# A hybrid decoder layer in fp32 on one core: residual loaded early, raw weights cut four slots behind their loads, output operands in pieces, leftover scores finished beside the first value tiles

## The chip, the cores and the metric

The kernel runs on one core of one Trainium2 chip. The time is the device time of one execution in microseconds (us), and the smaller it is the better. Three executions took 1523.22, 1521.63 and 1522.43 us, with a median of 1522.43 us. A fourth execution was recorded by the hardware profiler; it took 1521.24 us, and its trace spans 1519.5 us. All rows that are shown below come from that one.

## The reference

One decoder layer works on `x` of 1024 tokens by 1024 columns, with 256 memory tokens. Everything is float32. Two groups of heads run side by side on the same normalized input, and their outputs are joined before one output projection:

```python
h = rmsnorm(x, ln1)
z = h @ w_in                       # 4 mLSTM heads of 128, 8 attention heads of 64
mq, mk = silu(causal_conv(ml_qk))  # mLSTM: chunks of 64 tokens with a carried state
ml_out = norm(mlstm_chunkwise(mq, mk, mv, ig, lf)) * ml_norm * sigmoid(ml_o)

def block(qi, ci, blk):            # forgetting attention, 128 queries at a time
    s = q @ k.T * scale + (c[:, None] - c[None, :])   # c: running sum of log forget gates
    s = where(qpos >= kpos, s, -inf)
    return softmax(s) @ v

x = x + concat([ml_out, fx_out]) @ w_out
x = x + cross_attention(rmsnorm(x, ln_x), rmsnorm(mem, ln_mem), w_xq, w_xkv, w_xo)
u = relu(rmsnorm(x, ln2) @ w_ff1)
x = x + (u * u) @ w_ff2
return rmsnorm(x, ln_f)
```

## The kernel before

**Tiling.** The 1024 tokens are held as two halves of 512. Every float32 operand of a large product is kept as two parts, a rounded high part and the rest (`split`, L138 on ACT for the high part, L139 on DVE for the rest), and each product is three matmuls (`mm3`, L192 to L194). Weights come from memory unsplit into a ring of two buffers called `wr` ("raw") and are then cut into `wh` and `wl`.

**Engines and queues.** PE multiplies and transposes. ACT, DVE and POOL do the element work. All DMAs are issued by the queue of SP, in order, and an issue that has to wait for its data or its buffer holds back those behind it. A scheduler places the instructions of each engine, except inside `in_order(...)`, where the order of the source is kept.

**The stage of the change.** It computes the forgetting attention of the 8 heads, and lies between about 355 and 590 us of the trace. Its loop is `slot()` (L998). Scores of a head come in parts of at most 512 keys for 128 queries. A part goes through four steps: `score` (two matmuls, L754 and L755, into one of three PSUM banks called `sc`, with a causal mask added by L734 in the next slot), `top` (the maximum, DVE L761), `exp` (ACT L767, and for a second part also L769) and `scale` (the division by the sum, POOL L778). A value tile goes through `turn` (up to four transposes on PE, L793), `cut` (split of the transposed tile, L138 and L139) and `add` (matmuls with the values, L813). Each head's values are read back from DRAM by `fv_load` (L856, tile `w` from `fvd`), where `fv_sink` has stored them (L664).

The first 13 slots (`LEAD_`) do score parts only, without values. Then comes `token_major(w_fv)`, the projection of the values, in two passes of eight token tiles. Then about 96 slots do one value tile each, and in source order: turn, mask of the last score, add of the tile of two slots ago, `top` of the last score part, `cut`, `exp` of the part before that, `scale`, one waiting load (`fx_step`, L728), the next `score`, a stretch of filler matmuls, and at most one half of a raw weight cut (`cut_half`: ACT L971, then L972 on POOL for the first half and on DVE for the second). A score part needs the bank of the part three before it, and so the `exp` of that part.

**The filler.** `units` is a list of products that need nothing of this stage: key units and value units of the cross-attention's memory tokens (operand `hm`, 2 MB, read from `hmd` at L1074), then out units, the part of the output projection that needs only the mLSTM heads and the first attention heads. `cut_half` cuts the raw weights of the units ahead, as soon as fewer than three are waiting; after the second half of a raw weight it issues the load of the next one (L959) into the buffer that came free. The residual (`kept`, the first half of `x`, eight pieces of 256 KB) and the output operands (`mix_ahead`) are loaded piece by piece by `fx_step`, from a list `coming` that `score_parts` fills head by head. The output operands of the last heads (`mix_fx`, L877) are loaded behind the slots, in transfers of 768 KB.

Of the kernel before, what the change touches and what calls it, by code (L numbers as in the profile page):

```python
# [9 lines left out]
F32 = mybir.dt.float32  # L10
F32R = mybir.dt.float32r
AF = mybir.ActivationFunctionType
ALU = mybir.AluOpType
# [6 lines left out]
TH = 512  # L20
D = 1024
KT = D // P
NM = 256
MLH = 4
FXH = 8
# [3 lines left out]
KX = 1  # L29
# [15 lines left out]
def hybrid_layer(ctx: ExitStack, tc: tile.TileContext, a: dict, out: bass.AP):  # L45
    nc = tc.nc
    v, s, g = nc.vector, nc.scalar, nc.gpsimd
# [14 lines left out]
    def act(dt=F32R):  # L62
        return sb("act", [P, 8, TH], 7, dt)
# [47 lines left out]
    load = nc.sync.dma_start  # L111
# [35 lines left out]
    @contextmanager  # L147
    def in_order(engines=COMPUTE):

        traced = nc.cur_bb.bb.instructions  # L150
        last = traced[-1]
        yield
        start = next(k for k in reversed(range(len(traced))) if traced[k] is last) + 1
        for i in traced[start:]:
            if i.engine not in engines:
                continue
            if i.engine in last_of:
                tc.add_manual_dep(
                    i,
                    last_of[i.engine],  # L160
                    mybir.DependencyInfo(mybir.DependencyClass.NoSync, mybir.DependencyReason.DATA),
                    reason="in_order",
                )
            last_of[i.engine] = i.name
# [120 lines left out]
    hmd = dram.tile([P, 2, KT, NM], F32, name="hmd")  # L285
# [217 lines left out]
    def token_major(w_src, sink, cs=(0, 1), between={}, ready=()):  # L503

        for c in cs:
            ws = [both(ready.pop(0) if ready else weights(w_src[c, i]), lambda t: t.rearrange("p (k c) -> p k c", k=4)) for i in range(2)]
            for t in range(8):
                if t in between:
                    between[t]()
                hf, tt = divmod(t, 4)  # L510
                ps = mm()[:, 0:256]
                for k in range(KT):
                    x = both(h[hf], lambda z: z[:, k, tt * P : (tt + 1) * P])
                    mm3(ps, x, both(ws[k // 4], lambda z: z[:, k % 4]), k == 0, k == KT - 1)
                sink(t, c, ps)
# [150 lines left out]
    closing = iter(())  # L666
# [45 lines left out]
    coming = []  # L712
# [121 lines left out]
    def score_parts():  # L834

        for hd in range(FXH):
            for hf in range(2):
                if hf:
                    t = act(F32).rearrange("p a b -> p (a b)").rearrange("p (i c) -> p i c", i=4)
                    rooms[hd, hf] = [t[:, d, : (5 + d) * P] for d in range(4)]  # L840
                else:
                    t = [w4((P, 2, TH)) for _ in range(2)]
                    rooms[hd, hf] = [t[d // 2][:, d % 2, : (1 + d) * P] for d in range(4)]
                for d in range(4):
                    x = Tile(hd, 4 * hf + d, rooms[hd, hf][d])
                    for e in range(len(x.parts)):
                        yield x, e
            if hd + 2 < FXH:
                fx_load(hd + 2)
            if hd == FXH - 2:  # L850
                extra[hd].extend(mix_ahead(1))
            coming.extend(extra[hd])

    def fv_load(hd):
        t = w4((P, 8, P), F32R)
        load(t.bitcast(F32), fvd[hd])  # L856
        return t

    def value_steps():
# [22 lines left out]
    def mix_ahead(hf):  # L882
        t = act().rearrange("p (e k) c -> p e k c", e=2)
        z = [z4()[:, :T].bitcast(F32R).rearrange("p (e c) -> p e c", e=2) for _ in range(KX)]
        mixes[hf] = [(t[:, 0, k], t[:, 1, k]) for k in range(MLH)] + [(y[:, 0], y[:, 1]) for y in z]
        return [(mixes[hf][k][p_], mix[hf, p_, :, k]) for k in range(MLH + KX) for p_ in range(2)]

    late = []

# [59 lines left out]
    units += [out_unit(hf, n) for hf in range(2) for n in range(KT)]  # L949

    sources = [(u, src) for u, (srcs, _) in enumerate(units) for src in srcs]
    raws_, cuts_, halves = [], {}, [0]

    def raw_load():
        n = len(raws_)
        if n < len(sources):
            src = sources[n][1]
            raw = sb("wr", [P, 1024], 2)[:, : src.shape[-1]]
            last_raw[:] = [load(raw, src)]  # L959
            raws_.append(raw)  # L960

    def cut_half():

        n, e = divmod(halves[0], 2)
        raw = raws_[n]
        c = raw.shape[-1]
        if e == 0:
            cuts_.setdefault(sources[n][0], []).append(tuple(sb(t, [P, 1024], 3, F32R)[:, :c] for t in ("wh", "wl")))
        hi, lo = cuts_[sources[n][0]][-1]
        c = slice(e * c // 2, (e + 1) * c // 2)  # L970
        s.activation(hi[:, c], raw[:, c], AF.Copy)  # L971
        (v if e else g).tensor_tensor(out=lo[:, c], in0=raw[:, c], in1=hi[:, c].bitcast(F32), op=ALU.subtract)  # L972
        halves[0] += 1
        if e:
            raw_load()
# [19 lines left out]

    stores, topped = [], []

    def slot(values, until):  # L998
        with in_order(COMPUTE + (mybir.EngineType.SP,) * (values or not until)):
            todo_ = late[:]  # L1000
            late.clear()
            closing = bool(ended)
            sums = []
            while ended:
                sums.append(fx_close(*ended[0]))
                hd, hf, _ = ended.pop(0)
                if hd % 2:
                    stores.append((hd, hf, True))
            x = next(steps_, None) if values else None
            if x:  # L1010
                x.turn()
            mask()

            while adds and not closing and len(adds) >= (LAG if x else 1):
                y = adds.pop(0)
                y.add()
                if y.last:
                    ended.append((y.hd, y.hf, y.ov))
                    break
            tops = scored[:]  # L1020
            scored.clear()
            for t, e in tops:
                t.top(e)
            if x:
                x.cut()
                adds.append(x)
            for f in sums:
                f()
            exps = topped[:]
            topped[:] = tops  # L1030
            for t, e in exps:
                t.exp(e)
            while exped:
                exped.pop(0).scale()
            exped.extend(t for t, e in exps if e == len(t.parts) - 1)
            fx_step()
            part = next(parts, None)
            if part:
                part[0].score(part[1])
                scored.append(part)  # L1040
            late.extend(filter(None, [f() for f in todo_]))
            if stores and stores[0][2]:
                stores[0] = (*stores[0][:2], False)
            elif stores:
                fx_store(*stores.pop(0)[:2])
            while spent[0] < until:
                step = next(fill, None)
                if step is None:
                    break
                spent[0] += step[0]  # L1050
                if step[1]:
                    late.append(step[2])
                    break
            n, e = divmod(halves[0], 2)
            if until and n < len(sources) and (e or sum(u >= now[0] for u, _ in sources[:n]) < 3):
                cut_half()
        return x

    fx_load(0)
# [3 lines left out]
    for i in range(LEAD_):  # L1063
        slot(False, 0)
        if i in (1, 11):
            next(closing, None)
    token_major(a["w_fv"], fv_sink, between={4: lambda: next(closing, None)})
    hm = act().rearrange("p a b -> p (a b)").rearrange("p (e k c) -> p e k c", e=2, k=KT)
    kept = act(F32)
    residual = [(kept[:, n], a["x"][:, n, :TH]) for n in range(KT)]  # L1070
    operands = mix_ahead(0)
    for hd, more in ((1, residual[:4]), (2, operands[:4]), (3, operands[4:8]), (4, operands[8:] + residual[4:6]), (5, residual[6:])):
        extra[hd].extend(more)
    load(hm.bitcast(F32), hmd)  # L1074
    banks[:] = ["mm", "m2"]
    raw_load()
    raw_load()
# [13 lines left out]
        if step[1]:  # L1091
            (step[2]() or (lambda: None))()
    banks[:] = ["mm", "tp", "m2", "tp"]
    mix_fx = [mix_load(MLH + KX, KT, hf) for hf in range(2)]
    h2 = [(act(), act()) for _ in range(2)]
    second_acc = [w2("b") for _ in range(2)]
    mix_done = []
# [636 lines left out]
```

## Time and profile before

| what | value |
|---|---|
| median of three executions | 1522.43 us (1521.63 to 1523.22) |
| the profiled execution, its span | 1521.24 us, 1519.5 us |
| PE busy | 1502.5 us, 99% of the span |
| DVE, ACT, POOL busy | 1103.0, 716.8 and 441.5 us |
| moved by DMA | 288.32 MB, mean 190 GB/s |
| mean granted clock of PE | 0.996 |
| PE busy in 40 us from 360, 400, 440, 480, 520, 560 us | 38.88, 38.77, 37.64, 39.37, 40.00, 39.72 us |

The profile has for each instruction its start, its duration, its line, and in brackets the idle time of its engine ahead of it with the instruction that ended it. Rows of matmuls overlap: the next begins before the row of the one before it ends. A row of `SPq` is the issue of a DMA by SP's queue, not the transfer. In the rows of windows, each engine has its busy time in us and its instructions in brackets, and the last three columns are the granted clock of PE (1.00 is full), the busy share of the 16 DMA engines, and GB/s.

### The profile page before, as it was taken

The page shows a single profiled execution, that of the slowest core. Times are in us where ns is not written, and L with a number is a line of the kernel's source. Part 1 is how long each engine was busy: PE and PEld are TensorE (multiplying, and loading weights), DVE is VectorE, ACT ScalarE, POOL GpSimd, SP SyncE. Part 2 cuts the span into 40 slices and gives each one's busy share as a digit, 9 for nine tenths or more (in the row PEclk, how much of TensorE's full clock was granted, in tenths as well). Part 3 has the DMA queues.
Part 4 walks back from the last instruction along what each step waited for, and adds up shares of the span by engine and source line. Part 5 has one row for each costly group of instructions (what it writes and reads, how often), then busy time and mean ns, then how long its engine had stood idle before and what let it go on. Part 6 is the DMA issues. An engine that isn't in the chain of part 4 may idle for free.

```text
span 1519.5 us, 21816 instructions
## 1 busy us (share of the span) xinstructions
PE 1502.5 (99%) x7708; PEld 1260.7 (83%) x7708; DVE 1103.0 (73%) x1741; ACT 716.8 (47%) x1345; POOL 441.5 (29%) x497
## 2 busy tenths in 40 slices
PE   9999999999999999999999999999999999999997
PEld 8888888889898887888888888788888788888887
DVE  7666676665798875844457888788887788777765
ACT  7343343334677763543443456566556432222134
POOL 0003030413455541011110033344333544343312
PEclk9999999999999999999999999999999999999998
DMA  6332333446788858634333436776776966565623
GB/s 212 117 114 87 120 103 116 132 128 180 229 263 241 246 162 320 219 105 131 126 108 127 162 124 241 271 277 238 272 253 214 364 260 221 222 221 218 253 84 111
DMA packets 115217, 288.32 MB, mean 190 GB/s; under 512 B 12818, under 2 KB 27468, under 8 KB 109476
## 3 DMA queue, kind: packets, MB, share of 16 engines
q1 hardware_dynamic: 114820, 286.82, 55.9%
q8 instruction: 60, 0.98, 0.3%
q14 instruction: 49, 0.40, 0.1%
q10 hardware_dynamic: 288, 0.11, 0.0%
HBM read 194.36 MB, written 92.53 MB: 189 GB/s over the span
## 4 chain that ended last, share of the span: by engine, by line
PE 61%; DVE 3%; DMA 2%; issue 1%; ACT 1%; POOL 1%; SPq 0%; POOLq 0%; DVEq 0%; ACTq 0%
PE sc L192 5%; PE sc L194 5%; PE sc L193 5%; PE tp L192 5%; PE tp L194 5%; PE tp L193 5%; PE m L192 4%; PE m L194 4%; PE m L193 4%; PE mm L192 4%; PE mm L193 4%; PE mm L194 4%; PE ov L192 2%; PE ov L194 2%; PE ov L193 2%; PE ov L813 1%
## 5 line engine op out<-in xcount | busy, mean ns | idle before, releaser
L193 PE MATMUL tp<-act,wh 128*128 128x512 f32 (+1 forms) x456 | 178.7, 392 | 0.0
L192 PE MATMUL tp<-act,wl 128*128 128x512 f32 (+1 forms) x456 | 178.5, 392 | 0.0
L194 PE MATMUL tp<-act,wh 128*128 128x512 f32 (+1 forms) x456 | 178.5, 392 | 0.0
L138 ACT ACTIVATE wh<-wr 128x1024 fp32r<-128x1024 f32 (+3 forms) x96 | 92.7, 966 | 97.5 <-PE tp L194 36.4
L192 PE MATMUL mm<-act,wl 128*128 128x512 f32 (+1 forms) x320 | 122.9, 384 | 0.3 <-DVE r_b L940 0.3
L193 PE MATMUL mm<-act,wh 128*128 128x512 f32 (+1 forms) x320 | 122.5, 383 | 0.0
L194 PE MATMUL mm<-act,wh 128*128 128x512 f32 (+1 forms) x320 | 122.2, 382 | 0.0
L192 PE MATMUL m<-act,wl 128*128 128x512 f32 (+1 forms) x312 | 119.7, 384 | 0.5 <-DVE wl L139 0.5
L139 DVE TENSOR_TENSOR wl<-wr,wh 128x1024 fp32r<-128x1024 f32 (+3 forms) x96 | 111.9, 1166 | 10.6 <-ACT wh L138 10.5
L194 PE MATMUL m<-act,wh 128*128 128x512 f32 (+1 forms) x312 | 119.1, 382 | 0.0
L193 PE MATMUL m<-act,wh 128*128 128x512 f32 (+1 forms) x312 | 118.9, 381 | 0.0
L192 PE MATMUL sc<-act,wl 128*128 128x512 f32 (+1 forms) x268 | 103.8, 387 | 0.0
L193 PE MATMUL sc<-act,wh 128*128 128x512 f32 (+1 forms) x268 | 103.6, 387 | 0.0
L194 PE MATMUL sc<-act,wh 128*128 128x512 f32 (+1 forms) x268 | 103.6, 387 | 0.0
L194 PEld LDWEIGHTS tp<-act,wh 128*128 128x128 f32 x456 | 85.7, 188 | 19.5
L192 PEld LDWEIGHTS tp<-act,wl 128*128 128x128 f32 x456 | 85.7, 188 | 18.9
L193 PEld LDWEIGHTS tp<-act,wh 128*128 128x128 f32 x456 | 85.8, 188 | 18.8
L1468 POOL TENSOR_TENSOR z<-wr 128x256 f32<-128x256 f32 x56 | 53.5, 975 | 146.7 <-DMA wr<-w_ff2q 119.0
L138 ACT ACTIVATE w<-wr 128x768 fp32r<-128x768 f32 (+2 forms) x31 | 25.5, 825 | 130.1 <-PE tp L194 69.0
L138 ACT ACTIVATE wh<-z 128x1024 fp32r<-128x1024 f32 (+2 forms) x55 | 52.5, 956 | 65.6 <-POOL z L1468 30.6
L139 DVE TENSOR_TENSOR wl<-z,wh 128x1024 fp32r<-128x1024 f32 (+2 forms) x55 | 67.3, 1223 | 11.3 <-ACT wh L138 11.3
L194 PEld LDWEIGHTS mm<-act,wh 128*128 128x128 f32 x320 | 60.1, 188 | 12.5
(673 smaller groups left out, 4205.3 us busy)
## 6 DMA issues: line engine op xcount, KB each, us to landing
act<-right SPq DMA_DIRECT2D x35, 1024.0 KB
right<-r_d SPq DMA_DIRECT2D x70, 256.0 KB
right<-w SPq DMA_DIRECT2D x56, 256.0 KB
wr<-w_ff2q SPq DMA_DIRECT2D x28, 512.0 KB
act<-fqk SPq DMA_DIRECT2D x48, 256.0 KB
wr<-w_in SPq DMA_DIRECT2D x20, 512.0 KB
wr<-w_ff SPq DMA_DIRECT2D x20, 512.0 KB
fqk<-r_p SPq DMA_DIRECT2D x32, 256.0 KB
```

What stands on the lines that cost most here:

```text
L138: s.activation(hi, src, AF.Copy)
L139: return v.tensor_tensor(out=lo, in0=src, in1=hi.bitcast(F32), op=ALU.subtract)
L192: nc.tensor.matmul(ps, w[1], x[0], start=first, stop=False, skip_group_check=more)
L193: nc.tensor.matmul(ps, w[0], x[1], start=False, stop=False, skip_group_check=more)
L194: nc.tensor.matmul(ps, w[0], x[0], start=False, stop=last, skip_group_check=more)
L813: nc.tensor.matmul(self.ov[:, c0:], self.fv[:, self.j], t[:, c0:], start=self.j == 0 and t is self.p[1], stop=self.last and t is self.p[0])
L1468: g.tensor_tensor(out=o, in0=x, in1=y, op=op)
```

## The change

There are six edits.

1. `score_steps` takes the steps `top`, `exp` and `scale` out of `slot`, and `catch_up` calls them without a new score, ahead of token tiles 0 and 2 in each of the two passes of `token_major(w_fv)`. The score parts that the first 13 slots leave unfinished get their mask, maximum, exponential and division there.
2. `raw_load` notes the slot in which a raw weight was asked for, and `slot` cuts it only from four slots later on (`SETTLE`). `cut_for`, which a unit calls when it begins, does not look at that.
3. The POOL half of `cut_half` becomes two instructions of half the width.
4. The residual is loaded as four pieces of 512 KB, put into `coming` right behind the projection of the values, instead of eight pieces of 256 KB among the loads of heads 1, 4 and 5.
5. `hm` is loaded in two halves of 1 MB; the second is issued behind the first `fv_load`.
6. The output operands of the last heads are taken into `coming` at the last head, eight pieces of 256 KB (`rest_ahead`); four pieces of 256 KB are left for the place where the transfers of 768 KB stood (`rest_last`).

```diff
+            if hd == FXH - 1:
+                extra[hd].extend(rest_ahead())
             coming.extend(extra[hd])
...
-        load(t.bitcast(F32), fvd[hd])
+        x = load(t.bitcast(F32), fvd[hd])
+        if hd == 0:
+            with tc.issue_after(x.ins):
+                load(hm[:, :, KT // 2 :].bitcast(F32), hmd[:, :, KT // 2 :])
...
+    def rest_ahead():
+        for hf in range(2):
+            mix_fx.append(act().rearrange("p (e k) c -> p e k c", e=2))
+        return [(mix_fx[hf][:, p_, k], mix[hf, p_, :, MLH + KX + k]) for hf in range(2) for k in range(KT - MLH - KX - 1) for p_ in range(2)]
+
+    def rest_last(hf):
+        k = KT - MLH - KX - 1
+        for p_ in range(2):
+            load(mix_fx[hf][:, p_, k].bitcast(F32), mix[hf, p_, :, MLH + KX + k])
+        return [(mix_fx[hf][:, 0, k], mix_fx[hf][:, 1, k]) for k in range(k + 1)]
...
+    SETTLE = 4
...
+            asked.append(slots[0])
...
-        (v if e else g).tensor_tensor(out=lo[:, c], in0=raw[:, c], in1=hi[:, c].bitcast(F32), op=ALU.subtract)
+        if e:
+            v.tensor_tensor(out=lo[:, c], in0=raw[:, c], in1=hi[:, c].bitcast(F32), op=ALU.subtract)
+        else:
+            m = c.stop // 2
+            for q in (slice(0, m), slice(m, c.stop)):
+                g.tensor_tensor(out=lo[:, q], in0=raw[:, q], in1=hi[:, q].bitcast(F32), op=ALU.subtract)
...
+    def score_steps():
+        tops = scored[:]
+        scored.clear()
+        for t, e in tops:
+            t.top(e)
+        yield
+        exps = topped[:]
+        topped[:] = tops
+        for t, e in exps:
+            t.exp(e)
+        while exped:
+            exped.pop(0).scale()
+        exped.extend(t for t, e in exps if e == len(t.parts) - 1)
+
+    def catch_up():
+        with in_order():
+            mask()
+            for _ in score_steps():
+                pass
...
-            if until and n < len(sources) and (e or sum(u >= now[0] for u, _ in sources[:n]) < 3):
+            if until and n < len(sources) and slots[0] >= asked[n] + SETTLE and (e or sum(u >= now[0] for u, _ in sources[:n]) < 3):
                 cut_half()
+            slots[0] += 1
...
-    token_major(a["w_fv"], fv_sink, between={4: lambda: next(closing, None)})
+    token_major(a["w_fv"], fv_sink, between={0: catch_up, 2: catch_up, 4: lambda: next(closing, None)})
...
-    residual = [(kept[:, n], a["x"][:, n, :TH]) for n in range(KT)]
+    coming.extend((kept[:, n : n + 2], a["x"][:, n : n + 2, :TH]) for n in range(0, KT, 2))
...
-    load(hm.bitcast(F32), hmd)
+    load(hm[:, :, : KT // 2].bitcast(F32), hmd[:, :, : KT // 2])
...
-    mix_fx = [mix_load(MLH + KX, KT, hf) for hf in range(2)]
+    mix_fx = [rest_last(hf) for hf in range(2)]
```

**ACT where the value slots begin.** A row is a line, an operation, what it writes, what it reads, and the shape; numbers behind names tell copies apart. L767 is the `exp` of a score part, L141 stores a value tile of the projection, L138 is the high part of a transposed tile. Before:

```order
L141 ACTIVATE r_p_3769<-mm_3744,rcol 128x4x64
L141 ACTIVATE r_c_3798<-tp_3773,rcol 128x4x64
L141 ACTIVATE r_b_3827<-m_585_3802,rcol 128x4x64
L138 ACTIVATE r_d_3850<-tp_3843 128x512
L767 ACTIVATE act_3246,c_den_3304<-sc_3311,c_mx_3303 128x512
L769 ACTIVATE c_mx_3303<-c_mx_3303 128x1
L138 ACTIVATE r_d_3868<-tp_3862 128x384
L767 ACTIVATE w_537_3329,c_den_3332<-sc_3333,c_mx_3331 128x128
```

The same place after the change:

```order
L141 ACTIVATE r_p_3780<-mm_3755,rcol 128x4x64
L767 ACTIVATE act_3246,c_den_3304<-sc_3311,c_mx_3303 128x512
L769 ACTIVATE c_mx_3303<-c_mx_3303 128x1
L767 ACTIVATE w_537_3329,c_den_3332<-sc_3333,c_mx_3331 128x128
L141 ACTIVATE r_c_3809<-tp_3784,rcol 128x4x64
L141 ACTIVATE r_b_3838<-m_585_3813,rcol 128x4x64
L138 ACTIVATE r_d_3860<-tp_3855 128x512
L138 ACTIVATE r_d_3876<-tp_3870 128x384
```

The last two leftover exponentials stand ahead of the last two tiles of the value projection, and no longer behind the first transposed tiles.

**ACT at the eleventh raw weight** (a half of `w_xv`; the high part of a raw weight is L971 before and L991 after). Before:

```order
L138 ACTIVATE r_d_4841<-tp_4829 128x512
L767 ACTIVATE act_4709,c_den_4785<-sc_4786,c_mx_4784 128x512
L971 ACTIVATE wh_4871<-wr_4765 128x512
L138 ACTIVATE w_832_4883<-tp_4875 128x512
L767 ACTIVATE act_4709,c_den_4785<-sc_4819,c_mx_4784 128x256
L769 ACTIVATE c_mx_4784<-c_mx_4784 128x1
L138 ACTIVATE r_a_4856<-r_a_4856 128x256
L971 ACTIVATE wh_4871<-wr_4765 128x512
```

The same place after the change:

```order
L138 ACTIVATE r_d_4852<-tp_4840 128x512
L767 ACTIVATE act_4718,c_den_4795<-sc_4796,c_mx_4794 128x512
L138 ACTIVATE w_830_4890<-tp_4882 128x512
L767 ACTIVATE act_4718,c_den_4795<-sc_4830,c_mx_4794 128x256
L769 ACTIVATE c_mx_4794<-c_mx_4794 128x1
L138 ACTIVATE r_a_4867<-r_a_4867 128x256
L991 ACTIVATE wh_4908<-wr_4775 128x512
L138 ACTIVATE r_d_4922<-tp_4913 128x384
```

The first half of that cut stands one slot later, behind the `exp` that it stood ahead of.

**SP's queue at the first load of values.** Before (L1074 loads `hm`, L664 stores values, L644 and L645 store attention operands, L261 and L637 are small rows of the mLSTM state):

```order
L664 DMA fvd<-r_c_3624 128x4x128
L856 DMA w_593_3840<-fvd 128x1024
L261 DMA r_a_3215<-facd 128x512
L637 DMA r_d_3216<-facd 128x512
L664 DMA fvd<-r_b_3653 128x4x128
L664 DMA fvd<-r_p_3682 128x4x128
L1074 DMA act_3831<-hmd 128x4096
```

The same part of the queue after the change, up to the second half of `hm`:

```order
L664 DMA fvd<-r_p_3693 128x4x128
L644 DMA mix<-r_y_3316 128x512
L1112 DMA act_3842<-hmd 128x2x1024
L644 DMA mix<-r_e_3475 128x512
L645 DMA mix<-r_f_3067 128x512
L645 DMA mix<-r_f_2932 128x512
L664 DMA fvd<-r_c_3722 128x4x128
L664 DMA fvd<-r_b_3751 128x4x128
L664 DMA fvd<-r_p_3780 128x4x128
L858 DMA w_593_3851<-fvd 128x1024
L861 DMA act_3842<-hmd 128x2x1024
```

The first load of values (L856, now L858) moves from behind the ninth store of values to behind the fourteenth.

More of the change, by code (lines that the diff above doesn't have):

```diff
@@ L886, in mix_ahead @@
         return [(mixes[hf][k][p_], mix[hf, p_, :, k]) for k in range(MLH + KX) for p_ in range(2)]
+    mix_fx = []
+    def rest_ahead():
[7 more added lines that the diff above has]
+        return [(mix_fx[hf][:, 0, k], mix_fx[hf][:, 1, k]) for k in range(k + 1)]
     late = []
@@ L951, in hybrid_layer @@
     sources = [(u, src) for u, (srcs, _) in enumerate(units) for src in srcs]
-    raws_, cuts_, halves = [], {}, [0]
+    raws_, cuts_, halves, asked, slots = [], {}, [0], [], [0]
+    SETTLE = 4
     def raw_load():
@@ L1019, in slot @@
                     break
[L1020 to L1023, printed above, removed]
+            going = score_steps()
+            next(going)
             if x:
@@ L1028, in slot @@
                 f()
[L1029 to L1035, printed above, removed]
+            next(going, None)
             fx_step()
@@ L1066, in hybrid_layer @@
             next(closing, None)
-    token_major(a["w_fv"], fv_sink, between={4: lambda: next(closing, None)})
+    token_major(a["w_fv"], fv_sink, between={0: catch_up, 2: catch_up, 4: lambda: next(closing, None)})
     hm = act().rearrange("p a b -> p (a b)").rearrange("p (e k c) -> p e k c", e=2, k=KT)
     kept = act(F32)
-    residual = [(kept[:, n], a["x"][:, n, :TH]) for n in range(KT)]
+    coming.extend((kept[:, n : n + 2], a["x"][:, n : n + 2, :TH]) for n in range(0, KT, 2))
     operands = mix_ahead(0)
-    for hd, more in ((1, residual[:4]), (2, operands[:4]), (3, operands[4:8]), (4, operands[8:] + residual[4:6]), (5, residual[6:])):
+    for hd, more in ((2, operands[:4]), (3, operands[4:8]), (4, operands[8:])):
         extra[hd].extend(more)
-    load(hm.bitcast(F32), hmd)
+    load(hm[:, :, : KT // 2].bitcast(F32), hmd[:, :, : KT // 2])
     banks[:] = ["mm", "m2"]
```

## The prediction

> **What bounds the kernel now.** I read the engines' busy times first.
>
> ```profile
> PE 1502.5 (99%) x7708; PEld 1260.7 (83%) x7708; DVE 1103.0 (73%) x1741; ACT 716.8 (47%) x1345; POOL 441.5 (29%) x497
> ```
>
> PE is busy for 1502.5 of 1519.5 us, and the change takes no matmul away. It can only win time in which PE stands idle or runs slowly, inside the stage that it touches. So next come PE's waits between 360 and 600 us (what waited, for what: us in total, times, longest) and three windows of that stretch.
>
> ```profile
> PE sc L754 <- ACT act L767: 3.1, 2, 2.4
> PE tp L793 <- DVE r_e L139: 1.5, 2, 0.9
> PE sc L754 <- ACT w L767: 0.4, 1, 0.4
> PE mm L192 <- DVE r_b L940: 0.3, 1, 0.3
> PE tp L793 <- DVE w L139: 0.3, 1, 0.3
> ```
>
> ```profile
> 360.00:400.00 40.00, 38.88 (x311) 36.77 (x310) 26.22 (x71) 21.69 (x58) 13.29 (x20) 1.00 0.87 259
> 400.00:440.00 40.00, 38.77 (x292) 36.31 (x291) 37.23 (x83) 31.84 (x87) 20.91 (x30) 1.00 0.67 202
> 440.00:480.00 40.00, 37.64 (x273) 35.39 (x272) 31.83 (x78) 29.17 (x84) 20.32 (x31) 0.96 0.88 251
> ```
>
> The waits add up to 5.6 us in seven stalls. A stall costs a little more than its bracket shows:
>
> ```profile
> 410.20 0.28 PE L193 MATMUL mm<-wl,act 128*128 128x256 f32 x1
> 410.32 0.28 PE L194 MATMUL mm<-wh,act 128*128 128x256 f32 x1
> 411.47 0.33 PE L793 MATMUL tp<-ident,act 128*128 128x128 f32 x1 [0.87 <-DVE r_e L139]
> ```
>
> The row of 410.20 lasts 0.28 us, but the next starts after 0.12. Without the stall the row of 411.47 would have started at 410.44, and it came 1.03 later: 0.16 more than shown. I add 0.16 to each stall, 7 x 0.16 = 1.1 in all. Only the third window has a clock below 1.00. Its cause is the one long stall:
>
> ```profile
> 449.50 0.53 SPq L959 DMA_DIRECT2D wr<-w_xv  x1
> 457.41 0.63 ACT L971 ACTIVATE wh<-wr 128x512 fp32r<-128x512 f32 x1 [4.31 <-DMA wr<-w_xv]
> 459.03 0.50 PE L754 MATMUL sc<-act 128*128 128x512 f32 x1 [2.36 <-ACT act L767]
> 460.00:461.00 1.00, 1.00 (x8) 1.00 (x7) 0.98 (x2) 1.00 (x3) 0.00 (x0) 0.52 0.00 0
> 461.00:462.00 1.00, 1.00 (x4) 0.81 (x4) 0.96 (x4) 0.87 (x4) 0.00 (x0) 0.50 1.12 295
> 462.00:464.00 2.00, 2.00 (x11) 1.81 (x11) 1.45 (x5) 0.84 (x4) 1.60 (x3) 0.64 0.80 255
> ```
>
> ACT, in its order, stands 4.31 us at a raw half whose load took 7.9 us from issue to use; PE waits 2.36 for the exponential behind it, and right after that runs at 0.52, 0.50 and 0.64. At full clock that work had needed 0.48 + 0.50 + 2 x 0.36 = 1.7 us less. So the most that the change can win is 5.6 + 1.1 + 1.7 = 8.4 us, 0.55%.
>
> **The change part by part.**
>
> *Leftover scores.*
>
> ```profile
> 392.36 0.68 ACT L767 ACTIVATE act<-sc,c_mx 128x512 f32<-128x512 f32 x1
> 393.18 0.44 PE L754 MATMUL sc<-act 128*128 128x384 f32 x1 [0.73 <-ACT act L767]
> 396.99 0.38 PE L754 MATMUL sc<-act 128*128 128x256 f32 x1 [0.39 <-ACT w L767]
> 385.00:390.00 5.00, 5.00 (x45) 5.00 (x44) 1.99 (x6) 1.18 (x4) 1.48 (x3) 1.00 1.03 348
> ```
>
> The first value slots each wait for an exponential of a part that was left over from the slots without values. The change puts these ahead of the last projection tiles, where ACT is busy for 1.18 of 5 us, so they cost nothing there. It frees 0.73 + 0.39 + 2 x 0.16 = 1.4. Ends: 1.4, and 0 if the wait goes to the next link of the same chain. I take 1.2, near the first, since ACT's next work in these slots is only the high part of a transposed tile.
>
> *Four slots between load and cut.* The 96 value slots lie between about 394 us and the last stall at 585 us (below): 2.0 us each. The cut of the eleventh raw weight moves one slot, 2.0 us, and ACT would then wait 4.31 - 2.0 = 2.3. In the trace 4.31 of ACT's waiting cost PE 2.36, so 1.95 are slack, and 0.35 + 0.16 = 0.5 stay. Stalls of 0.73 and 0.87 left the clock at 1.00 in their windows, so the 1.7 go too. The gain is 2.36 + 0.16 + 1.7 - 0.5 = 3.7. Its ends are 4.2 (the load comes sooner) and 0 (it comes later still). What speaks for sooner is that the transfers of the residual ahead of it are gone:
>
> ```profile
> 432.91 1.39 SPq L728 DMA_DIRECT2D act<-x  x3
> 400.00:405.00 5.00, 5.00 (x41) 4.71 (x39) 4.65 (x7) 4.70 (x13) 2.20 (x3) 1.00 0.40 123
> ```
>
> They now go at about 402 to 412 us, where the DMA engines are 0.40 busy, as four issues in place of eight. They cost nothing there; if that cover were gone, they would delay the raw load that follows in the same queue, which has four slots in hand.
>
> *The POOL half in two pieces, and cuts moved off the 410 stall.*
>
> ```profile
> 408.06 1.29 POOL L972 TENSOR_TENSOR wl<-wr,wh 128x512 fp32r<-128x512 f32 x1
> 408.38 1.25 DVE L139 TENSOR_TENSOR r_p<-r_p 128x256 fp32r<-128x256 f32 x1
> 409.56 0.68 DVE L972 TENSOR_TENSOR wl<-wr,wh 128x512 fp32r<-128x512 f32 x1
> 491.97 0.42 DVE L139 TENSOR_TENSOR r_p<-r_p 128x256 fp32r<-128x256 f32 x1 [0.31 <-ACT r_p L138]
> L972 POOL TENSOR_TENSOR wl<-wr,wh 128x512 fp32r<-128x512 f32 x16 | 21.7, 1358 | 6.5 <-ACT wh L971 5.4 <-issue 1.1
> L603 POOL TENSOR_TENSOR r_b<-r_c,r_b 128x256 f32<-128x256 f32 x16 | 15.6, 976 | 6.1 <-DVE r_c L599 5.4
> ```
>
> While POOL ran its half, a DVE subtraction of 256 columns took 1.25 instead of 0.42, and the DVE half of the same cut, 0.68, came behind it. PE then waited 0.87 for DVE. This cut moves two slots later with the four-slot rule, so both rows leave this place; of 1.03 I take 0.8 and leave 0.2 for where they land. Ends: 1.03 and 0.
>
> The other two stalls behind DVE are 1.5 - 0.9 = 0.6 and 0.3 in the list, with 2 x 0.16 together 1.2. Pieces of 256 columns are not in the trace for this line. Half of 1358 ns is 0.68 each and 976 ns is the nearest row of that width, so a pair costs POOL 1.4 to 1.95 in place of 1.36; POOL is busy for 21 of 40 us and nothing in PE's waits names it. A DVE instruction is then held by at most 0.68 to 0.98. I take half of the 1.2, 0.6; ends 1.2 and 0.
>
> [...]
>
> *Output operands in pieces.*
>
> ```profile
> 578.95 5.52 DMA r_b<-x
> 585.40 0.47 PE L192 MATMUL mm<-act,wl 128*128 128x512 f32 x1 [0.28 <-DVE r_b L940]
> 560.00:570.00 10.00, 10.00 (x60) 8.39 (x59) 6.21 (x15) 5.72 (x14) 5.03 (x7) 1.00 0.27 79
> ```
>
> In the chain that ended last, a residual piece (`r_b`) took 5.52 us behind two transfers of 768 KB, and PE waited 0.28. Two thirds of the operands now go at about 557 to 577 us, where the DMA engines are 0.27 busy. The stall goes: 0.44; ends 0.44 and 0.
>
> *The first load of values moves back behind five more stores.*
>
> ```profile
> 377.65 0.45 SPq L1074 DMA_DIRECT2D act<-hmd  x1
> 387.88 0.53 SPq L664 DMA_DIRECT2D fvd<-r_p  x1
> 393.84 0.48 PE L813 MATMUL ov<-r_e,w 128*128 128x512 f32 x1
> 401.89 0.35 SPq L959 DMA_DIRECT2D wr<-w_xk  x1
> 405.34 0.63 ACT L971 ACTIVATE wh<-wr 128x512 fp32r<-128x512 f32 x1 [0.43 <-DMA wr<-w_xk]
> act<-hmd SPq DMA_DIRECT2D x1, 2048.0 KB
> act<-fqk SPq DMA_DIRECT2D x48, 256.0 KB
> ```
>
> It is now issued behind the store of 387.88, at about 388.4. The first use, at 393.84, moves up by the stall that is gone, to 392.95. A transfer of the same 512 KB took 3.4 us with a free DMA (401.89 to 405.34) and 7.9 with a busy one (the raw weight above), so it lands between 391.8 and 396.3, and PE waits 0 to 3.35 us. Just here the DMA is full (1.03), which is nearer to the second. But 1 MB of the 2 MB of `hm` and three attention operands of 256 KB that stood ahead of this place in the queue now follow the load; at 348 GB/s that is 5 us of queue. So I take the first end, and a cost of 0.
>
> *New stalls.* The moved cuts put four halves into consecutive slots late in the stage (60 to 63), and one filler unit cuts its second half only as it begins. No row shows this. It is bounded by nothing and by one long stall with its clock (4.2); nearest is the stall of 0.87 behind DVE, and I take 1.0.
>
> **The sum.** 1.2 + 3.7 + 0.8 + 0.6 + 0.44 + 0 - 1.0 = 5.7 us less. The profiled execution took 1521.24, so 1515.5. It lies 1.2 below the median; I add 0.5, as I don't know how the next median lies: **1516.0**.
>
> **The rivals.**
> - *The eleventh raw weight is still late.* Its 7.9 us are a matter of what the DMA carries, and one slot is 2.0 us. If it lands 2 us later still, stall and clock stay: 1516.0 + 3.7 = 1519.7. Against it stands the residual that left the queue. Chance 0.12.
> - *The two pieces hold DVE as long as one did.* Then 0.6 and half the 0.8 are lost: 1517.0. Chance 0.10.
> - *Stalls move.* DVE is busy for 37.23 of 40 us from 400 on; what PE wins ahead of that, DVE may take back. The gains at 392 to 410 and the 0.6 go (2.6): 1518.6. Chance 0.13.
> - *The first load of values is late.* At the far end above PE waits 3.35 and the clock falls as it did after 2.36: 3.35 + 0.16 + 1.7 = 5.2, which gives 1521.2. It becomes slower than before by 3 us only from a wait of some 7.6 us on, so if the load lands after 400.6, 12 us after its issue: 1526. The full DMA speaks for it; that no 512 KB took over 7.9 us in these rows speaks against. Chance 0.10 for that.
> - *No effect.* Each moved cut makes a stall like the one it left: 1521.5. Chance 0.11.
>
> **How the numbers follow.** The forecast itself has 0.44, with a range of its own from 1514.4 (all gains at their upper ends) to 1517.5 (half of the terms beside the long stall lost). A measurement can tell about 0.2%, 3 us, from no change. Below 1519.4 lie the forecast, the second and the third rival and half of the first: 0.73. Within 3 us lie the other half and no effect: 0.17. Slower: 0.10. The range runs from 1513.0, all that can be won from the median with 1 us to spare, to 1521.5, which leaves out the late load alone.
>
> **What would show it.** PE's wait of 2.36 gone and a clock of 1.00 from 440 to 480 us; no wait of PE for L767 at 392 and 397; ACT's wait for the raw half under 2.3; PE's waits for DVE under 0.6 in all; the residual piece landing within 4 us of its issue near 579. I am wrong if PE waits at its first value matmul (L813) for the load of values, or if ACT's waits for raw weights stay as long as they were.

## The result, and the profile after

The changed kernel takes 1515.17 us (median of five executions, 1514.37 to 1516.89), against 1521.63 us (1519.48 to 1523.22) for the kernel before. The ratio is 0.9967, with a 95% interval from 0.9956 to 0.9979. The forecast was 1516.0 in a range of 1513.0 to 1521.5. The profiled execution took 1514.53 us with a span of 1512.8, so its span is 6.7 us shorter than before.

PE's waits between 360 and 600 us after the change (what waited, for what: us in total, times, longest), and the three windows that were shown of before:

```profile
PE sc L754 <- ACT act L767: 0.8, 1, 0.8
PE tp L793 <- DVE r_e L139: 0.4, 1, 0.4
```

```profile
360.00:400.00 40.00, 39.57 (x319) 37.59 (x318) 26.60 (x71) 22.02 (x60) 13.67 (x22) 1.00 0.78 229
400.00:440.00 40.00, 39.17 (x297) 36.92 (x296) 35.71 (x86) 32.64 (x90) 23.98 (x38) 1.00 0.94 276
440.00:480.00 40.00, 39.88 (x299) 37.52 (x298) 35.38 (x86) 32.27 (x90) 23.03 (x39) 1.00 0.95 261
```

The waits fell from 5.6 to 1.2 us and from seven to two, and the clock is at 1.00 in all three windows. By the prediction's own way of counting this is 4.4 + 5 x 0.16 + 1.7 = 6.9 us, and the span says 6.7. The time from the first score to the last (first and last start in the rows of L754) fell from 206.6 to 200.5 us. The first row is of before, the second of after:

```profile
L754 PEld LDWEIGHTS sc<-act x96: 186/188/330, 350.6 to 557.2; 128*128 128x128 f32 x96
```

```profile
L754 PEld LDWEIGHTS sc<-act x96: 186/188/200, 351.1 to 551.6; 128*128 128x128 f32 x96
```

The two waits that are left in the changed kernel, and rows that stand beside them (`...` marks rows that are left out):

```profile
393.91 0.33 PE L793 MATMUL tp<-ident,w 128*128 128x128 f32 x1 [0.43 <-DVE r_e L139]
394.17 0.48 PE L813 MATMUL ov<-r_e,w 128*128 128x512 f32 x1
...
424.78 0.33 SPq L978 DMA_DIRECT2D wr<-w_xk  x1
434.01 0.63 ACT L991 ACTIVATE wh<-wr 128x512 fp32r<-128x512 f32 x1 [2.81 <-DMA wr<-w_xk]
435.53 0.39 PE L754 MATMUL sc<-act 128*128 128x256 f32 x1 [0.83 <-ACT act L767]
455.91 0.63 ACT L991 ACTIVATE wh<-wr 128x512 fp32r<-128x512 f32 x1 [0.97 <-DMA wr<-w_xv]
```

At 393.91 the third value tile waits for the split of the first, a new wait at the place where the leftover exponentials were moved away. The first matmul with values, at 394.17, does not wait for their load. At 434 a raw weight, the eighth, is 9.2 us from issue to use, and the DMA share of the window from 400 to 440 us rose from 0.67 to 0.94; ACT stands 2.81 us and PE 0.83. At the eleventh raw weight ACT now waits 0.97 in place of 4.31, and PE's list has no wait there. ACT's waits for raw weights did not vanish. In the cuts of 512 columns they add up to 4.6 us, against 5.4 before; they stand at other weights, and cost PE less. The first row is of before, the second of after:

```profile
L971 ACT ACTIVATE wh<-wr 128x512 fp32r<-128x512 f32 x32 | 20.2, 633 | 5.4 <-DMA wr<-w_xv 4.3 <-DMA wr<-w_xk 1.1
```

```profile
L991 ACT ACTIVATE wh<-wr 128x512 fp32r<-128x512 f32 x32 | 20.2, 635 | 4.6 <-DMA wr<-w_xk 3.6 <-DMA wr<-w_xv 1.0
```

### The profile page after: what moved, and what is told of

It reads as the page before. It is cut to its first block, busy times and chain, and to the rows that moved or that the text cites. A ratio compares the mean times of both kernels' runs of the same rounds, so it can differ in the third digit from the quotient of the medians.

```text
span 1512.8 us, 21863 instructions
## 1 busy us (share of the span) xinstructions
PE 1499.7 (99%) x7708; PEld 1258.8 (83%) x7708; DVE 1097.8 (73%) x1741; ACT 716.5 (47%) x1345; POOL 449.1 (30%) x529
## 4 chain that ended last, share of the span: by engine, by line
PE 89%; DMA 4%; DVE 3%; issue 1%; ACT 1%; POOL 1%; SPq 0%; POOLq 0%; DVEq 0%; ACTq 0%
PE tp L193 8%; PE tp L194 8%; PE tp L192 8%; PE sc L192 6%; PE sc L194 6%; PE sc L193 6%; PE m L192 6%; PE m L194 6%; PE m L193 6%; PE mm L192 6%; PE mm L193 6%; PE mm L194 6%; PE ov L192 2%; PE ov L193 2%; PE ov L813 2%; PE ov L194 2%
## 5 line engine op out<-in xcount | busy, mean ns | idle before, releaser
L138 ACT ACTIVATE wh<-wr 128x1024 fp32r<-128x1024 f32 (+3 forms) x96 | 92.7, 966 | 97.6 <-PE tp L194 37.9
L138 ACT ACTIVATE w<-wr 128x768 fp32r<-128x768 f32 (+2 forms) x31 | 25.5, 825 | 130.6 <-PE tp L194 69.1
L138 ACT ACTIVATE wh<-z 128x1024 fp32r<-128x1024 f32 (+2 forms) x55 | 52.5, 955 | 65.9 <-POOL z L1506 27.1
```

The source lines that it names most:

```text
L138: s.activation(hi, src, AF.Copy)
```

## The experiments

All but one are the changed kernel with one or two things different. Their ratios are against the kernel before, run beside them on the same chip; the changed kernel's own is 0.9967. The kernel before took 1520.18 to 1520.47 us beside them and 1521.63 us beside the changed kernel, so kernels are to be compared by their ratios. Each trace is of one execution.

| kernel | median us | ratio to before, 95% interval |
|---|---|---|
| four slots taken away (0) | 1523.41 | 1.0014 [1.0004, 1.0025] |
| two slots | 1522.86 | 1.0018 [1.0007, 1.0028] |
| six slots | 1531.89 | 1.0074 [1.0061, 1.0088] |
| the four slots alone, on the kernel before | 1515.39 | 0.9964 [0.9951, 0.9978] |
| residual late | 1514.41 | 0.9959 [0.9946, 0.9973] |
| residual late and 0 slots | 1521.87 | 1.0007 [0.9996, 1.0019] |
| residual at head 4 | 1513.83 | 0.9963 [0.9950, 0.9976] |
| residual at head 4, no leftover scores | 1515.21 | 0.9961 [0.9948, 0.9974] |
| leftover scores not finished early | 1514.67 | 0.9956 [0.9943, 0.9968] |
| hm in one load | 1515.94 | 0.9973 [0.9962, 0.9983] |
| POOL half in one instruction | 1515.65 | 0.9969 [0.9957, 0.9981] |
| output operands whole | 1514.85 | 0.9961 [0.9949, 0.9974] |

### What took the long stall away: four slots, or the residual's new place

```diff
-    SETTLE = 4
+    SETTLE = 0
```

> The changed kernel with no slots between load and cut (0 in place of 4); the residual stays early. Theory A, the four slots took the long stall away: ACT waits some 4 us again for the eleventh raw weight, PE some 2 us for the exponential behind it, the clock falls to about 0.5 for 3 us, and the time is 1515.2 + 3.7 = 1518.9. Theory B, the long stall went because the residual left the queue ahead of that load: PE's waits in the stage stay under 2 us in all, the clock stays at 1.00, and the time is 1515 to 1516.5.

Measured: 1523.41 us, slower than the kernel before, and 0.47% above the changed kernel's ratio. PE's waits for the exponentials in the stage, the issue of the fourth raw weight, and ACT's two longest waits for raw weights:

```profile
PE sc L754 <- ACT act L767: 6.6, 3, 5.1
```

```profile
402.08 0.36 SPq L978 DMA_DIRECT2D wr<-w_xk  x1
411.25 0.63 ACT L991 ACTIVATE wh<-wr 128x512 fp32r<-128x512 f32 x1 [6.16 <-DMA wr<-w_xk]
461.99 0.63 ACT L991 ACTIVATE wh<-wr 128x512 fp32r<-128x512 f32 x1 [3.32 <-DMA wr<-w_xv]
```

Theory A holds for the time, and by more than it said, but at another place. The longest stall is not at the eleventh raw weight but at the fourth, which took 9.2 us from issue to use. In the trace of before the same load, issued at 401.89, was in use after 3.4. In the changed kernel it was issued at 401.63 and in use at 408.79, after 7.2 us, and ACT waited 0.79 for it. So the other edits make this load late, and the four slots hide that too.

```diff
-    coming.extend((kept[:, n : n + 2], a["x"][:, n : n + 2, :TH]) for n in range(0, KT, 2))
+    residual = [(kept[:, n], a["x"][:, n, :TH]) for n in range(KT)]
...
-    for hd, more in ((2, operands[:4]), (3, operands[4:8]), (4, operands[8:])):
+    for hd, more in ((1, residual[:4]), (2, operands[:4]), (3, operands[4:8]), (4, operands[8:] + residual[4:6]), (5, residual[6:])):
```

> The changed kernel with the residual in eight pieces at the heads 1, 4 and 5, as before; the four slots stay. Theory A: the long stall stays away, and the new stall of 0.8 us at 434 goes, because the load of the raw weight there no longer lands 9.2 us after its issue: 1514.2. Theory B: ACT waits for the eleventh raw weight again by 2 us or more, PE by 2 with the clock: 1517 to 1519.

Measured: 1514.41 us; the wait of 0.83 at 434 is gone, as theory A said, but there is 1.4 at the fourth raw weight and 1.0 at the eleventh:

```profile
PE sc L754 <- ACT act L767: 2.4, 2, 1.4
456.67 0.63 ACT L991 ACTIVATE wh<-wr 128x512 fp32r<-128x512 f32 x1 [1.89 <-DMA wr<-w_xv]
```

So theory B, that the long stall comes back, falls; the two smaller stalls together, 2.4 us, are more than the one that went. The time does not tell the early residual from the late one.

> The changed kernel with both undone. Both theories: the long stall of about 2.4 us and the fall of the clock come back, 1518.5 to 1519.5. If either alone has them back already, this one adds nothing to that run.

Both undone give 1521.87 us, 2.4 us above the expected end; PE waits 6.2 us for L767 (two stalls, the longer 3.4), behind 4.37 us of ACT's waiting at the fourth weight and 4.84 at the eleventh. Against the run with 0 slots and the residual early (3.32) ACT's wait at the eleventh weight is longer by 1.5 us; with the slots it is 1.89 and 0.97, so these change it by 2.4 to 3.0. The residual is late here, and the fourth weight is late all the same, so the residual is not what delays that one.

### The four slots alone

```diff
--- before.py
+    SETTLE = 4
...
+            asked.append(slots[0])
...
-            if until and n < len(sources) and (e or sum(u >= now[0] for u, _ in sources[:n]) < 3):
+            if until and n < len(sources) and slots[0] >= asked[n] + SETTLE and (e or sum(u >= now[0] for u, _ in sources[:n]) < 3):
                 cut_half()
+            slots[0] += 1
```

> The kernel before with nothing but the four slots between load and cut. Theory A, these carry most of the change: PE's waits for the exponential behind the eleventh raw weight fall from 2.4 to about 1.0 us, as with the residual late, the clock stays at 1.00, the stall of 0.87 at 411 goes; 3.5 to 4.5 us less than before. Theory B, the four slots only pay for what the other edits of the load queue cost: less than 1.5 us less than before.

Measured: 1515.39 us against 1520.18 beside it, 4.8 us less. By the ratios (0.9964 and 0.9967) that is as much as the whole change brings. Its waits and the window of the long stall:

```profile
PE sc L754 <- ACT act L767: 0.7, 1, 0.7
PE tp L793 <- DVE w L139: 0.7, 1, 0.7
PE sc L754 <- ACT w L767: 0.4, 1, 0.4
PE mm L192 <- DVE r_b L940: 0.3, 1, 0.3
440.00:480.00 40.00, 39.88 (x300) 37.51 (x299) 35.58 (x87) 32.66 (x91) 22.28 (x34) 1.00 0.96 269
```

```profile
L973 ACT ACTIVATE wh<-wr 128x512 fp32r<-128x512 f32 x32 | 20.2, 633 | 0.8 <-DMA wr<-w_xv 0.8
456.10 0.63 ACT L973 ACTIVATE wh<-wr 128x512 fp32r<-128x512 f32 x1 [0.80 <-DMA wr<-w_xv]
```

The long stall, the fall of the clock and the 0.87 at 411 are gone with this edit alone. ACT's waits for raw weights in the cuts of 512 columns are 0.8 us in all, against 5.4 before and 4.6 in the changed kernel, so the other edits bring back most of what the slots take away. The 0.80 stand at the eleventh weight, with the residual late as before; with the residual late in the changed kernel it was 1.89, so this wait differs by 1 us between two kernels that both have the residual late. The four waits that are left to PE, 2.1 us, are those at which the other edits aim. These edits take them away and bring 1.2 of their own. Of the 0.9 us that is left between the two lists, the profiled spans (1513.0 and 1512.8) show 0.2. The trace of after has 1.9 us of waits outside the stage that the trace of this kernel does not name.

### How many slots

> The changed kernel with two slots between load and cut in place of four. A slot is 2.0 us and a raw weight takes 7 to 9 us to land where the queue is full. If the wait follows from that difference, ACT's waits for raw weights lie between those with 0 slots (10.5 us) and with 4 (4.6), PE's waits between 7.0 and 1.2, and the time is 1517 to 1521. If any spacing is enough: 1515.2.

> The changed kernel with six slots in place of four. The cover for late loads grows by 4 us, so ACT's waits for raw weights (4.6 us) vanish; but several filler units now begin before their weight is cut, both halves are then cut back to back ahead of PE, and PE waits 1 to 2 us at each of some five units: 1518 to 1524. Rival: the scores between hide that, and the time is 1514.4, without the stall near 434.

Two slots: 1522.86 us, no better than none. The forecast was 1517 to 1521. The profiled execution took the least of twelve (1516.86; the others 1520.55 to 1526.95). In its trace ACT's waits for raw weights (8.7 us) and PE's waits (4.5 us) lie between the others as expected, but it does not stand for the median. Nine of the other eleven have a mean granted clock of 0.994 or 0.995 against its 0.997, so falls of the clock are likely part of what it lacks; where they stand, no trace shows.

Six slots: 1531.89 us, 8 us beyond the forecast's end. The direction and the mechanism were right, the size was not:

```profile
PE mm L192 <- POOL wl L997: 7.1, 6, 2.5
PE mm L193 <- POOL wl L997: 4.1, 3, 2.7
451.28 1.87 POOL L997 TENSOR_TENSOR wl<-wr,wh 128x256 fp32r<-128x256 f32 x2 [1.00 <-ACT wh L991]
452.06 0.58 PE L192 MATMUL mm<-act,wl 128*128 128x256 f32 x1 [2.51 <-POOL wl L997]
```

ACT's waits for raw weights in the slots are gone, but units begin uncut. Then ACT, POOL and PE work one behind the other, and POOL's pieces, 1.87 us for two, are on the path. Nine waits for POOL cost 11.2 us. The expectation also left out the clock: in this trace it is at 0.50 from 421.1 to 424.5, from 451.8 to 455.2 and from 499.6 to 506.4 us (0.96, 0.96 and 0.91 in the windows of 40 us from 400, 440 and 480). PE is busy for 12.7 us of that, which at full clock would take 6.3 us less. So the spacing has two sides, and four is between them.

### Leftover scores, `hm`, POOL pieces, output operands

```diff
-    token_major(a["w_fv"], fv_sink, between={0: catch_up, 2: catch_up, 4: lambda: next(closing, None)})
+    token_major(a["w_fv"], fv_sink, between={4: lambda: next(closing, None)})
```

> The changed kernel without the steps that finish leftover scores beside the last value projections. As the prediction has it: PE waits again for L767 at the first value tiles, 0.73 and 0.39 us, and the time is 1515.2 + 1.4 = 1516.6. Rival: without these steps the first load of values stands early in SP's queue again, the queue behind 388 us is shorter by 512 KB, and ACT's wait of 0.79 us for the raw weight at 409 goes; what PE loses at 392 is paid back and the time stays at 1515.2.

Measured: 1514.67 us. The waits of 0.73 and 0.39 are back, and the one of 0.43 at 394 and the 0.83 at 434 are gone; one of 0.7 at the eleventh weight has come (ACT waits 1.64 there). ACT no longer waits at the fourth raw weight. The rival holds. PE's waits and the group of ACT's cuts of 512 columns (`w_xk` 1.1; with the early scores it was 3.6):

```profile
PE sc L754 <- ACT act L767: 1.5, 2, 0.7
PE sc L754 <- ACT w L767: 0.4, 1, 0.4
L991 ACT ACTIVATE wh<-wr 128x512 fp32r<-128x512 f32 x32 | 20.2, 635 | 2.7 <-DMA wr<-w_xv 1.6 <-DMA wr<-w_xk 1.1
```

In its order the first load of values stands behind the ninth store again, and both halves of `hm` right behind the eleventh. The early scores are what moved that load behind five more stores. The wait at the fourth raw weight goes with them too. The four traces without them (this one, the one with the residual at head 4, the four slots alone, the kernel before) have at most 0.43 us of ACT's waiting there. Those with them have 0.79 to 6.16 us, except the kernels with `hm` in one load and with six slots, which have none.

```diff
-    load(hm[:, :, : KT // 2].bitcast(F32), hmd[:, :, : KT // 2])
+    load(hm.bitcast(F32), hmd)
```

> The changed kernel with hm in one load of 2 MB ahead of the first load of values. If the second half behind that load is needed: another 1 MB at about 340 GB/s, 3 us, stands ahead, the values land near 395.9 us in place of 392.9, PE waits at its first L813 for the DMA by about 1.7 us, and the time is about 1517. If the load of values had slack enough: no wait at L813, 1515.2.

Measured: 1515.94 us, and the wait that was foretold, with a fall of the clock behind it:

```profile
PE ov L813 <- DMA w<-fvd: 1.4, 1, 1.4
394.58 0.64 PE L813 MATMUL ov<-r_e,w 128*128 128x512 f32 x1 [1.37 <-DMA w<-fvd]
360.00:400.00 40.00, 38.20 (x291) 35.77 (x292) 25.36 (x67) 19.88 (x56) 12.03 (x19) 0.96 0.81 245
```

So the second half of `hm` behind the values is what keeps this wait away, once the early scores have moved the load of the values; the time alone does not show it.

```diff
-            for q in (slice(0, m), slice(m, c.stop)):
+            for q in (c,):
```

> The changed kernel with the POOL half of a raw cut in one instruction. If pieces relieve DVE: DVE's subtraction of 256 columns (r_p, r_a) is back at about 0.65 us from 0.42, the DVE half of the cut at 0.93 from 0.84, PE waits for DVE by 0.5 to 1.2 us more, and the time is 1515.8 to 1516.4. If two pieces hold DVE as long as one: no wait of PE differs by over 0.3 us and the time is 1515.2.

Measured: 1515.65 us, just under the first expectation and not to be told from 1515.17. The instructions do tell. DVE's half of the cut and its subtraction of 256 columns, in one POOL instruction and then in two (the changed kernel):

```profile
PE tp L793 <- DVE w L139: 0.7, 1, 0.7
L993 DVE TENSOR_TENSOR wl<-wr,wh 128x512 fp32r<-128x512 f32 x15 | 14.0, 933 | 2.1 <-ACT wh L991 1.9
L139 DVE TENSOR_TENSOR r_p<-r_p 128x256 fp32r<-128x256 f32 x4 | 1.9, 482 | 0.0
```

```profile
L993 DVE TENSOR_TENSOR wl<-wr,wh 128x512 fp32r<-128x512 f32 x15 | 12.6, 839 | 1.8 <-ACT wh L991 1.6
L139 DVE TENSOR_TENSOR r_p<-r_p 128x256 fp32r<-128x256 f32 x4 | 1.7, 432 | 0.9 <-ACT r_p L138 0.9
L997 POOL TENSOR_TENSOR wl<-wr,wh 128x256 fp32r<-128x256 f32 x32 | 25.8, 826 | 5.2 <-ACT wh L991 2.3 <-PE m L192 1.2 <-issue 1.1
```

Against what the first expectation said, the subtraction went back to 482 ns only, not 650. DVE's half falls from 933 to 839 ns, and PE's wait of 0.7 behind DVE goes. A pair of pieces costs POOL 1.65 us, in place of 1.36. There is something else in the trace with one POOL instruction: the residual is early there, but PE has no wait near 434, and one behind the fourth raw weight instead:

```profile
412.32 0.38 PE L754 MATMUL sc<-act 128*128 128x256 f32 x1 [1.42 <-ACT act L767]
```

So which raw weight comes late for PE changes even with an edit that leaves the order of SP's queue as it is.

```diff
-    mix_fx = [rest_last(hf) for hf in range(2)]
+    mix_fx = [mix_load(MLH + KX, KT, hf) for hf in range(2)]
```

(`rest_ahead` is taken out with it.)

> The changed kernel with the last output operands in four loads of 768 KB behind the slots, as before. As the prediction has it: the residual piece near 579 takes 5 us or more again and PE waits about 0.3 us for it: 1515.2 + 0.44 = 1515.6. Rival: the piece is not waited for any more, since the rest of the stage has shifted against it: 1515.2.

Measured: 1514.85 us. The wait comes back, and the time doesn't show it:

```profile
579.84 0.47 PE L192 MATMUL mm<-act,wl 128*128 128x512 f32 x1 [0.34 <-DVE r_b L956]
```

### A third place for the residual

```diff
-    for hd, more in ((2, operands[:4]), (3, operands[4:8]), (4, operands[8:])):
+    for hd, more in ((2, operands[:4]), (3, operands[4:8]), (4, operands[8:] + residual)):
```

> The changed kernel with the four residual loads of 512 KB put behind the output operands of head 4, near 505 us, where the first use is at 512 to 517 us. If the two stalls behind late raw weights (0.8 us near 434 with the residual early, 1.0 near 457 with it late) both come from the residual's place in the queue, neither is there, and the time is about 1 us under the changed kernel, 1514.0 to 1514.4. Rival: the transfers that stay are enough to make either weight late, or the residual delays raw weights near 505: 1515 or more.

> The same without finishing leftover scores beside the value projections. PE waits 0.73 and 0.39 us for L767 at the first value tiles, and not 0.4 for DVE at the second: 0.8 us more than with it, unless the earlier load of values saves as much: 1514 to 1515.

Neither is faster than the changed kernel by more than the intervals. With the early scores the times spread from 1511.77 to 1521.53, and the profiled execution lies near the upper end (1520.38). There the wait near 434 is gone, but not the one at the eleventh weight: ACT waits 1.93 us there and PE 1.06. The fourth raw weight was 1.8 us late for PE, and a small load of the next head 1.5 us:

```profile
535.53 0.36 PE L754 MATMUL sc<-act 128*128 128x256 f32 x1 [1.48 <-DMA act<-decay]
```

Without the early scores PE waits 0.73 and 0.38 at the first value tiles, as foretold, and not at the fourth weight. No version here beats the changed kernel, or the four slots alone, by more than can be measured.

## Why the prediction was right, and where it was not

**The time and the sum.** 1515.17 against 1516.0. The sum was 5.7 us, and the trace gives 6.9 by the same counting. The long stall with its clock gave 4.2 in place of 3.7, since no wait was left behind it. The stall at 411 gave 1.03 in place of 0.8 and the other two waits for DVE 1.2 in place of 0.6, but the first value tiles only 0.85 in place of 1.2.

**The four slots (3.7 + 0.8 = 4.5).** Right in kind and nearly in size: alone they are worth 4.8 us. The step that failed is smaller: "1.95 are slack, and 0.35 + 0.16 = 0.5 stay". The slack (ACT's waiting that costs PE nothing) belongs to the place of the cut. Where the cut stood before, 4.31 and, with no slots, 3.32 us of ACT's waiting cost PE 2.36 and about 1.3; one slot later 1.89 cost 1.0, 1.64 cost 0.75, and 0.97 no wait that the list names. That is 2.0 in the one place and 0.9 in the next. It was made up for by a shorter wait: I had put 2.3 for ACT, and in the traces with four slots it was 0.3 to 1.9, or not in the list at all. That the two errors offset each other is luck. The shorter wait does not need the residual out of the queue, as I had argued: with the four slots alone the residual is late, and ACT waits 0.80.

**The residual "cost nothing there".** This is not settled. With it at 407 to 413 us the eighth raw weight was late, 0.83 us at 434, and with it late that wait was gone. But it was gone as well with the residual early and the early scores undone, and with the residual early and one POOL instruction (a wait of 1.42 at the fourth weight in its place). So the residual alone does not decide it.

**The first load of values (0).** Right: no wait. That it hangs on the halved `hm` was shown by 1.4 us of waiting without it. What I did not count is what the same queue does to the weights behind it: the fourth raw weight took 9.2 us with no slots, against 3.4 before. The four slots hide that, so taking them away costs about 7 us, more than the change gains. The wait at this weight goes with the early scores; whether it is the moved load of values or the half of `hm` behind it that delays the weight, no run tells.

**Leftover scores (1.2), pieces (0.6), output operands (0.44).** Undoing each brings back a wait of the kind it was counted for: 0.73 and 0.39, 0.7, 0.34. But a wait of 0.43 came behind the first, and of the two waits that I gave to the pieces, the one of 0.6 is gone with the four slots alone. Undoing any one of the three does not move the time by what can be told. The gain of the change is the four slots; that these add to it is not shown.

**New stalls (1.0).** The size was right, 0.83 + 0.16, and the place wrong: not slots 60 to 63 with their four halves, but the eighth raw weight. That the size fits is luck.

**The signs.** The clock, the wait of 2.36, the waits at 392 and 397, ACT's wait at the eleventh weight (0.97) and PE's waits for DVE (0.4) came out as named. Two did not. The residual piece near 579 (now issued at 573.46) was used after 4.7 us and not within 4, though PE has no wait for it:

```profile
578.16 0.69 DVE L958 TENSOR_TENSOR r_b<-mm,r_b 128x512 f32<-128x512 f32 x1 [1.39 <-DMA r_b<-x]
```

And ACT's waits for raw weights, which were to show me wrong if they stayed as long, fell only from 5.4 to 4.6 us in the cuts of 512 columns. By this sign the whole change hardly worked. The four slots did: alone they leave 0.8. The other edits bring 3.8 back, which PE feels little, because the slack at their places covers most: 0.79 and 0.97 cost PE nothing, and 2.81 cost it 0.83.

**The rivals.** The eleventh weight still late: no, as said. The two pieces holding DVE as long as one: no, 839 ns against 933. That they might was an estimate of mine, which no row of before showed. Stalls that move: the 0.43, and ACT's waits as said. No effect and the late load of values: no.

## What to carry to other kernels

Where an engine works in order, don't let it ask for a transfer that may not have landed: leave a fixed number of steps between the issue and the use, and count what is queued behind the waiting instruction. In this kernel the number had two sides (0 and 2 slots: 1523; 4: 1515; 6: 1532), since a step that comes too late is done on the path of its consumer. An edit of a load queue should be priced by every load behind it, and small waits that are taken away one by one need not add up in the time.

## What was not expected of the hardware

The fall of PE's clock is not set by the length of a wait alone. In the kernel before, the wait of 2.36 us was followed by 3.4 us at half clock. With two slots a wait of 2.70 us (the longest of its list) was followed by none. The stretch before the fall and the fall itself in the kernel before, then the stretch with the wait of 2.70 us and the one behind it with two slots:

```profile
456.63:460.04 3.41, 1.05 (x7) 0.92 (x7) 1.14 (x3) 2.63 (x8) 1.28 (x2) 1.00 0.59 198
460.04:463.46 3.42, 3.42 (x14) 3.03 (x13) 3.35 (x9) 2.66 (x8) 1.06 (x2) 0.50 0.66 189
```

```profile
406.00:410.00 4.00, 1.30 (x8) 0.78 (x7) 1.27 (x3) 2.44 (x7) 1.86 (x3) 1.00 0.85 277
410.00:414.00 4.00, 4.00 (x32) 3.82 (x31) 3.80 (x11) 3.63 (x12) 1.45 (x4) 1.00 0.66 189
```

With `hm` in one load the wait of 1.37 us, with the 0.43 ahead of it, was enough. With no slots the clock fell within the wait of 5.13 us and stayed at half for twice 3.41 us, 4.5 us of it after the work had begun again:

```profile
391.38:394.79 3.41, 1.61 (x12) 1.08 (x11) 2.77 (x6) 1.88 (x5) 0.00 (x0) 1.00 1.06 274
394.79:398.20 3.41, 3.41 (x11) 2.77 (x11) 0.96 (x3) 0.84 (x3) 0.49 (x3) 0.50 1.09 294
```

```profile
410.60:414.01 3.41, 1.14 (x3) 0.94 (x4) 1.27 (x3) 2.76 (x8) 1.42 (x2) 0.50 0.26 102
414.01:417.42 3.41, 3.41 (x15) 3.22 (x14) 3.01 (x8) 1.81 (x7) 1.18 (x3) 0.50 0.66 185
```

All nine stretches at half clock between 380 and 580 us of the fourteen traces last 3.4 us (six) or 6.8 us (three). In the windows of 40 us they show as six clocks of 0.96 and three of 0.91.

PE was busy for 1.05 and 1.61 of the 3.41 us ahead of two of the falls, in the kernel before and with `hm` in one load. With two slots it was busy for 1.30 of the 4.00 us from 406, and no fall followed. What decides it besides the length of a wait is not shown, as no run moves a wait and leaves the rest. The 1.7 us of clock that I counted with the long stall (half of the 3.42 us of busy PE at 0.50) were right for that execution, but another wait of the same length need not cost them.
